# Which engine makes the low halves of weights in two sparse attentions

## The chip, the cores and the metric

The kernel runs on one core of a Trainium2 chip. The metric is the device time of one execution in microseconds (us). TensorE multiplies; ScalarE, VectorE and GpSimd prepare its operands and evacuate its results; loads and stores are issued from SyncE's queue. In the profile the engines are called PE (its weight loads PEld), ACT, DVE, POOL and SP.

## The reference

Three layers work on a sequence of 512 rows of 1024 numbers, in float32. The first two (a latent attention with its feed-forward part, a gated recurrence with its own) are not touched. The third takes a normed input h, projects it once with a wide matrix and feeds three mixers: a sparse attention that keeps 256 keys a query, chosen by a small indexer; a sparse attention over compressed, selected and windowed keys; and a state-space mixer. Each mixer's output is multiplied by a branch matrix and gated:

```python
u = h @ w_in[l]
y_a = dsa_mixer(...)      # top-k: lax.top_k(idx, n_sel), softmax over the chosen keys
y_b = nsa_mixer(...)      # 2 groups of 8 heads, three softmaxes each
y_c = ssd_mixer(...)
gates = jax.nn.sigmoid(mg.reshape(bsz, seq, 3, D_MODEL))
mix = (gates[:, :, 0] * (y_a @ w_br_dsa[l]) + gates[:, :, 1] * (y_b @ w_br_nsa[l])
       + gates[:, :, 2] * (y_c @ w_br_ssd[l]))
x = x + mix @ w_out[l]
```

## The kernel before

Every large product is made of three, so that float32 accuracy is kept: both operands are split into a high half, rounded to the matmul's input type, and a low half, the rest. `mm3` (lines 122 to 126) multiplies high by high, high by low and low by high; these are lines 124, 125 and 126 of the profile. Weights are split on the chip. `raw` (line 183) loads a piece from memory, `chunk` (line 203) makes its halves:

```python
self.nc.scalar.copy(w[:, 0], raw)
(self.nc.gpsimd if self.late and LP else self.lo).tensor_sub(w[:, 1], raw, w[:, 0])
```

So ScalarE converts (line 209), and the engine that `self.lo` names subtracts (line 210). A chunk has 128 x 1024 numbers in nearly all cases. `self.lo` also names the engine of the subtraction in `split_pair` (line 628, 128 x 512), which splits an attention's output, and of one addition in `fill_out` (line 1265), which is not reached for the first branch.

`block2` (line 1192) runs the third layer. While an attention works, TensorE also multiplies "fills": projections that a later part needs. A fill tile is one chunk, 24 products on TensorE and an evacuation. `dense_a` with `fill=True` marks its loads, chunks and evacuations as urgent: they are placed in the engines' orders as if they stood 1000 instructions earlier (`SOON`), as far as buffers allow: 3 raw pieces (`FWR`) and 2 split chunks (`FWC`). So a fill's chunk is made about two tiles ahead of its use. The order of the instructions on each engine is fixed when the program is built.

The stages around the change, in order:

- `dsa` (line 1273), prelude: the indexer (queries and keys of it are split and transposed, lines 1299 to 1313; scores and ReLU, lines 1326 to 1333), top-k by 16 rounds of MAX8 and MATCH_REPLACE for each of three blocks (lines 1336 and 1337) closed by line 1338, and `queries` for two halves of the heads (4 chunks each; transposes at line 1180). 8 of 16 gate tiles are filled ahead of the heads (`DG = 8`).
- `dsa`, heads: 16 heads in 8 pairs, each with 4 scores, a masked minimum on VectorE (line 572), exponentials on ScalarE (line 574), transposes, splits and products with the values (`pv2`). After each of the first 8 heads follows a gate tile. Each pair ends in `split_pair`.
- `nsa_group` (line 1426), run for two groups: a prelude (projection, `normed_keys` with transposes at line 1155, compression at lines 1474 to 1480, queries, the selection of blocks up to line 1557), then the fills, then 8 heads. The fills of the first group are the 8 tiles of the first branch's projection (`fill_out`), those of the second 13 tiles of z (`fill_z`, `ZN = 13`).

In the second attention `self.lo` is set by the five numbers of `NV`. The first four choose it at four places of the prelude, by `EN(nc, 1 - NV[i])`: 1 is VectorE, 0 GpSimd. The fifth is the number of fills ahead of which `self.lo` is not yet GpSimd:

```python
for f in fill[:NV[4]]:
    f()
self.lo = nc.gpsimd
for f in fill[NV[4]:n]:
    f()
```

With `NV = 1, 1, 1, 0, 0` the chunks of both preludes' own projections and queries are VectorE's, and all fills GpSimd's. From line 1207 on, and so in the whole first attention, `self.lo` is GpSimd.

Of the kernel before, what the change touches and what calls it, by code (L numbers as in the profile page):

```python
# [34 lines left out]
class Kern:  # L35
# [1156 lines left out]
    def block2(self, X, right, xp):  # L1192
        nc, A = self.nc, self.A
        self.banks(*BATT)
        self.win = win = A["w_in_2"][0]
        self.win2 = win.rearrange("(k p) n -> p k n", p=128)
        dt = lambda n, name: [self.dram.tile([128, S], F32, name=name, tag=name, bufs=n) for _ in range(n)]
        self.gd, self.zd, self.rd = dt(24, "gd"), dt(16, "zd"), [dt(8, "ra"), dt(8, "rb")]
        with ExitStack() as left:

            first = []
            self.dense_b(lambda a, b: (self.win2[:, a:b, 1024:1448], self.win2[:, a:b, 8408:8440]), X, KD, 456,
                         lambda tb, p: first.append(p), early=EF)
            self.spill_h()
            self.main.close()
            self.X2 = X
            self.lo = nc.gpsimd
            self.big = self.pool("b2", 6, left)
            self.fl = self.pool("fill", 2, left)
            self.fwr, self.fwc = self.pool("fwr", FWR, left), self.pool("fwc", FWC, left)  # L1210
            with ExitStack() as att:
                self.time_steps(first)
                self.wr, self.wc = self.pool("awr", 2, att), self.pool("awc", 2, att)
                self.dsa(X, win, first)
                self.nsa(X, win)
            self.banks(*BSSD)
            yT, rb = self.ssd(X, win, xp)
            mxp = self.pool("mxp", 4, right, side="right")
            self.wr, self.wc = (self.pool(n, b, right, side="right") for n, b in (("wor", 2), ("woc", 4)))
            mx = self.ssd_out(yT, rb, mxp)  # L1220
            self.banks(4, 2, 0, 2)

        self.lo = nc.vector
        x2 = lambda shape, dt, name: xp.tile([128] + shape, dt, name=name, tag="b8")
        self.reload_h([x2([2, D], F32, "h") for _ in range(2)])
        with ExitStack() as st:
            self.big = self.pool("big2", 8, st)
            xn = []
            bridge = self.bridge(st, None, None, A["norm2_g_2"][0], None, lambda tb: xn[tb // 2][:, tb % 2])
            xn += [x2([2, D], F32, "xn") for _ in range(2)]  # L1230
            for a in range(2):
                self.run_section(A["w_out_2"][0], a * 4, lambda k, hl: mx[a][hl][:, k], 4, self.add_to(self.H, False, 0.5),
                                 (lambda: bridge) if a else None)
            self.mlp(bridge[2], A["w_ff1_2"][0], A["w_ff2_2"][0], None, None)
# [191 lines left out]
    def nsa_group(self, X, g, gk, pos, vis, anyv, keep, addc, ltm, fill):  # L1426
        nc, A = self.nc, self.A
        with ExitStack() as st:
# [10 lines left out]
            with ExitStack() as st2:  # L1439
# [24 lines left out]

                self.lo = EN(nc, 1 - NV[0])
                self.dense_b(wsrc, X, KD, 408, evac)
                self.lo = EN(nc, 1 - NV[1])
                self.normed_keys(ip, kraw, 2, NT, lambda i: gk[:, 1 + i], lambda i: kS[i][:, 0], lambda i: kL[i][:, 0])
# [23 lines left out]
            with ExitStack() as st2:  # L1492
                ip = self.pool("cmpa", 1, st2)
                self.lo = EN(nc, 1 - NV[2])
                self.queries(ip, 1448 + g * 512, qT)
                self.lo = EN(nc, 1 - NV[3])
                pc = ip.tile([128, NT, 8, 32], F32, name="pc", **sh(SH3, "qs", 2))
# [69 lines left out]
            n = len(fill) - (NF0, NF1)[g]  # L1567
# [5 lines that stand above are left out]
# [422 lines left out]
S4 = 0  # L1995
MPN = ()
MRG = 0, 1, 2, 3
NV = 1, 1, 1, 0, 0
SH1 = 1
SH2 = 1  # L2000
SH3 = 1
# [123 lines left out]
```

## Time and profile before

| | us |
|---|---|
| time, median of 3 runs | 2748.62 (2748.05 to 2750.14) |
| profiled execution: its own time | 2748.3 |
| profiled execution: its span, first to last instruction | 2746.6 |
| the two sparse attentions in it, roughly | 1280 to 1950 |
| TensorE busy | 2652.5 |
| VectorE busy | 1619.0 |
| ScalarE busy | 1204.4 |
| GpSimd busy | 498.6 |

Times in views count from the span's start. A busy TensorE is not TensorE at its peak, since its multiplications are pipelined. [...] Idle time of an engine that nobody waits for costs nothing.

### The profile page before, as it was taken

Reading aid. Unit: us, or ns where it says so; the run is one execution under the profiler, and the core shown is the slowest. Engines: PE = TensorE matmul, PEld = TensorE weight load, DVE = VectorE, ACT = ScalarE, POOL = GpSimd, SP = SyncE. Lnnn points to the kernel's source line nnn. Section 1 sums busy time; section 2 is a strip of 40 time slices with the busy share of each in tenths; the row PEclk is TensorE's granted clock in tenths of the full one; section 3 lists DMA queues with packets and bytes.
Section 4 is the critical chain, followed back from the end, with each engine's and each line's share of the span. In section 5 each row is a group of like instructions: output and inputs, shape, how many; then the busy total and the mean of one; then the engine's idle time right before and its main releaser. Section 6 shows DMA issues by size and latency. Waiting matters only on the chain. (4 is left out here: it accounts for less than half of the span.)

```text
span 2746.6 us, 35061 instructions
## 1 busy us (share of the span) xinstructions
PE 2652.5 (97%) x13329; PEld 2192.9 (80%) x13329; DVE 1619.0 (59%) x3211; ACT 1204.4 (44%) x2382; POOL 498.6 (18%) x373
## 2 busy tenths in 40 slices
PE   8999999999998999998999999999999999999999
PEld 6888888878887888886777777777788888788887
DVE  6755444455655444457966669659557773554444
ACT  5555323335454423234367438437556552332232
POOL 1010000020002000003322213212555557100000
PEclk9999999999999999999999999999999999999999
DMA  4232223312232332233231241221353335223322
GB/s 140 62 123 77 92 93 107 109 63 84 76 116 80 99 102 92 92 119 115 89 78 59 77 109 35 62 74 36 110 155 97 112 115 169 92 92 98 101 92 77
DMA packets 281966, 259.10 MB, mean 94 GB/s; under 512 B 39436, under 2 KB 224068, under 8 KB 281796
## 3 DMA queue, kind: packets, MB, share of 16 engines
q1 hardware_dynamic: 281796, 256.84, 30.2%
q8 instruction: 105, 1.72, 0.3%
q14 instruction: 65, 0.53, 0.1%
HBM read 234.79 MB, written 22.02 MB: 94 GB/s over the span
## 5 line engine op out<-in xcount | busy, mean ns | idle before, releaser
L124 PE MATMUL pm<-xT,wch 128*128 128x512 f32 (+1 forms) x1568 | 598.1, 383 | 3.1 <-ACT xT L129 1.5
L209 ACT CAST wch<-raw 128x1024 fp32r<-128x1024 f32 (+3 forms) x389 | 402.6, 1041 | 448.1 <-PE pm L126 349.8
L126 PE MATMUL pm<-xT,wch 128*128 128x512 f32 (+1 forms) x1568 | 596.4, 381 | 1.2 <-POOL wch L210 1.2
L125 PE MATMUL pm<-xT,wch 128*128 128x512 f32 (+1 forms) x1568 | 596.7, 381 | 0.9 <-DVE xT L130 0.9
L210 POOL TENSOR_TENSOR wch<-raw,wch 128x1024 fp32r<-128x1024 f32 (+3 forms) x127 | 308.2, 2433 | 673.1 <-ACT wch L209 624.0
L210 DVE TENSOR_TENSOR wch<-raw,wch 128x1024 fp32r<-128x1024 f32 (+1 forms) x262 | 320.2, 1225 | 184.7 <-ACT wch L209 183.8
L124 PEld LDWEIGHTS pm<-xT,wch 128*128 128x128 f32 x1568 | 296.3, 190 | 55.8 <-ACT xT L129 3.2
L126 PEld LDWEIGHTS pm<-xT,wch 128*128 128x128 f32 x1568 | 297.6, 190 | 53.5 <-POOL wch L210 1.6
L125 PEld LDWEIGHTS pm<-xT,wch 128*128 128x128 f32 x1568 | 297.6, 190 | 52.0 <-DVE xT L130 2.0
L124 PE MATMUL pm<-wch,hT 128*128 128x512 f32 x768 | 300.1, 393 | 0.0
L125 PE MATMUL pm<-wch,hT 128*128 128x512 f32 x768 | 296.5, 390 | 0.0
L126 PE MATMUL pm<-wch,hT 128*128 128x512 f32 x768 | 296.4, 390 | 0.0
L529 DVE SCALAR_TENSOR_TENSOR f<-pm,r 128x512 f32<-128x512 f32 x96 | 66.4, 691 | 243.1 <-ACT r L528 242.9
L528 ACT ACTIVATE r<-pm 128x512 f32<-128x512 f32 x96 | 57.4, 598 | 315.2 <-PE pm L126 315.2
L124 PEld LDWEIGHTS pm<-wch,hT 128*128 128x128 f32 x768 | 144.3, 188 | 36.4 <-ACT hT L530 7.1
L126 PEld LDWEIGHTS pm<-wch,hT 128*128 128x128 f32 x768 | 143.6, 188 | 30.8
L125 PEld LDWEIGHTS pm<-wch,hT 128*128 128x128 f32 x768 | 144.3, 188 | 29.3
L478 POOL TENSOR_TENSOR acc<-acc,g 128x512 f32<-128x512 f32 x16 | 22.5, 1404 | 689.6 <-ACT bj L462 689.6
L574 ACT ACTIVATE p<-p,mn 128x128 f32<-128x128 f32 x224 | 125.5, 564 | 20.5 <-DVE mn L572 19.5
L440 DVE TENSOR_TENSOR acc<-pm,acc 128x512 f32<-128x512 f32 x96 | 66.1, 689 | 99.5 <-PE pm L126 99.2
L130 DVE TENSOR_TENSOR pT<-pt,pT 128x512 fp32r<-128x512 f32 x224 | 100.1, 484 | 34.7 <-ACT pT L129 32.8
L129 ACT CAST pT<-pt 128x512 fp32r<-128x512 f32 x224 | 85.3, 427 | 44.8 <-PE pt L613 30.0
(568 smaller groups left out, 4822.6 us busy)
## 6 DMA issues: line engine op xcount, KB each, us to landing
raw<-in_mlp_w_dram SPq DMA_DIRECT2D x64, 1024.0 KB, 5.2
raw<-in_w_in_dram SPq DMA_DIRECT2D x64, 512.0 KB, 3.7
raw<-in_w_ff_dram SPq DMA_DIRECT2D x32, 1024.0 KB, 5.4
raw<-in_hgrn_w_in_dram SPq DMA_DIRECT2D x24, 512.0 KB, 4.1
raw<-in_w_in_dram SPq DMA_DIRECT2D x8, 1024.0 KB, 5.0
raw<-in_w_br_ssd_dram SPq DMA_DIRECT2D x16, 512.0 KB, 4.0
gd<-fo SPq DMA_DIRECT2D x24, 256.0 KB, 2.2
fg<-gd SPq DMA_DIRECT2D x24, 256.0 KB, 3.1
```

The source lines that it names most:

```text
L124: mm(p, ah, bh, start=start, stop=False)
L125: mm(p, ah, bl, start=False, stop=False)
L126: mm(p, al, bh, start=False, stop=stop)
L129: self.nc.scalar.copy(h, src)
L130: self.nc.vector.tensor_sub(l, src, h)
L209: self.nc.scalar.copy(w[:, 0], raw)
L210: (self.nc.gpsimd if self.late and LP else self.lo).tensor_sub(w[:, 1], raw, w[:, 0])
L440: self.nc.vector.tensor_add(d, p, d)
L478: (nc.vector if tb > BP else nc.gpsimd).tensor_mul(a[:, f], a[:, f], g1[:, f])
L528: nc.scalar.activation(r, p, AF.Relu)
L529: nc.vector.scalar_tensor_tensor(f, p, 0.0, r, op0=ALU.max, op1=ALU.mult)
L574: nc.scalar.activation(p, p, AF.Exp, bias=mn[:, b:b + 1], scale=-1.0, accum_out=sm[:, b:b + 1])
```

## The change

In the first attention `self.lo` becomes VectorE. In the second, the fourth place of the prelude chooses VectorE, and the first 8 fills of each group come ahead of the switch to GpSimd: all 8 tiles of the first group, 8 of 13 of the second. After the fills of each group `self.lo` is GpSimd as before, for the `split_pair` of the second attention's heads and for the state-space mixer.

```diff
@@ -1204,7 +1204,7 @@
             self.X2 = X
-            self.lo = nc.gpsimd
+            self.lo = nc.vector
             self.big = self.pool("b2", 6, left)
@@ -1995,7 +1995,7 @@
-NV = 1, 1, 1, 0, 0
+NV = 1, 1, 1, 1, 8
```

## Rows read from the trace of the kernel before

**Rows 1.** The page's part 1: busy us, share of the span and instructions of each engine.

```profile
PE 2652.5 (97%) x13329; PEld 2192.9 (80%) x13329; DVE 1619.0 (59%) x3211; ACT 1204.4 (44%) x2382; POOL 498.6 (18%) x373
```

**Rows 2.** Windows view by stage: busy us (x instructions) of each engine, PEclk, DMA share, GB/s.

```profile
1254.00:1400.00 146.00, 128.79 (x594) 103.79 (x595) 117.68 (x289) 63.50 (x127) 45.49 (x19) 0.95 0.37 109
1400.00:1540.00 140.00, 135.89 (x758) 108.88 (x757) 88.01 (x251) 98.45 (x254) 34.82 (x57) 1.00 0.18 50
1540.00:1650.00 110.00, 100.44 (x495) 81.22 (x495) 67.55 (x155) 39.03 (x76) 22.07 (x12) 0.92 0.42 116
...
1745.00:1785.00 40.00, 34.88 (x191) 27.76 (x190) 25.78 (x74) 15.71 (x37) 10.55 (x6) 0.96 0.35 105
```

**Rows 3.** Waits of TensorE, 1250 to 1780: us in total, times, longest.

```profile
PE pt L1180 <- DVE qs L1176: 6.0, 4, 2.2
PE pt L1155 <- ACT kp L1149: 5.7, 2, 3.1
PE pt L1307 <- DVE ry L153: 5.3, 1, 5.3
PE psc L1326 <- ACT rl L1328: 3.5, 2, 1.8
PE pt L1564 <- DVE pc L1540: 2.3, 1, 2.3
...
PE pt L1155 <- DVE kp L1150: 1.6, 1, 1.6
PE pt L1307 <- DVE rt L151: 1.3, 1, 1.3
PE psc L125 <- POOL wch L210: 1.3, 1, 1.3
PE psc L1480 <- DVE bl L1476: 1.2, 1, 1.2
PE pm L126 <- POOL wch L210: 1.2, 1, 1.2
```

**Rows 4.** Timeline of GpSimd: start us, us, line, operation, tiles, count, idle time before.

```profile
1288.17 7.25 POOL L210 TENSOR_TENSOR wch<-raw,wch 128x1024 fp32r<-128x1024 f32 x3 [4.23 <-ACT wch L209]
...
1359.03 2.38 POOL L210 TENSOR_TENSOR wch<-raw,wch 128x1024 fp32r<-128x1024 f32 x1 [11.52 <-ACT wch L209]
```

**Rows 5.** Timeline of VectorE at six places.

```profile
1287.36 0.15 DVE L151 TENSOR_TENSOR rt<-ry 128x4 f32<-128x4 f32 x1
...
1288.43 2.15 DVE L152 TENSOR_TENSOR rt<-rt,rx 128x4 f32<-128x4 f32 x1
...
1317.92 2.41 DVE L1333 SCALAR_TENSOR_TENSOR dm<-rl,iw,dm 128x384 f32<-128x384 f32 x1
...
1359.46 0.69 DVE L1336 MAX8 m<-dm 128x8 f32<-128x512 f32 x1
...
1376.15 1.86 DVE L1338 TENSOR_SCALAR dm<-dm 128x512 f32<-128x512 f32 x1
...
1770.81 2.34 DVE L1476 TENSOR_SCALAR bl<-kcs,pos 128x31 f32<-128x31 f32 x1
```

**Rows 6.** Groups by line: count, busy us, mean ns, idle; page, then 1250 to 1780.

```profile
L210 DVE TENSOR_TENSOR wch<-raw,wch 128x1024 fp32r<-128x1024 f32 (+1 forms) x262 | 320.2, 1225 | 184.7 <-ACT wch L209 183.8
...
L210 POOL TENSOR_TENSOR wch<-raw,wch 128x1024 fp32r<-128x1024 f32 (+1 forms) x42 | 101.2, 2416 | 266.1 <-ACT wch L209 229.9 <-issue 16.7 <-PE pt L1180 15.3
...
L130 DVE TENSOR_TENSOR pT<-pt,pT 128x512 fp32r<-128x512 f32 x32 | 22.1, 689 | 10.0 <-ACT pT L129 9.6
```

**Rows 7.** Windows view of two stretches of VectorE.

```profile
1309.00:1377.00 68.00, 61.88 (x270) 48.46 (x269) 67.00 (x168) 23.84 (x39) 23.21 (x10) 1.00 0.29 90
1651.00:1705.00 54.00, 52.52 (x310) 42.58 (x308) 52.02 (x182) 44.16 (x133) 17.57 (x15) 1.00 0.16 45
```

**Rows 8.** ScalarE's conversions, 1250 to 1780.

```profile
L209 ACT CAST wch<-raw 128x1024 fp32r<-128x1024 f32 (+1 forms) x52 | 52.9, 1019 | 41.2 <-PE po L126 27.1 <-PE pm L126 4.9 <-DMA raw<-in_w_in_dram 4.7
```

**Rows 9.** Waits of VectorE, 1250 to 1780.

```profile
DVE wch L210 <- ACT wch L209: 25.1, 7, 6.8
```

## The prediction

> **What bounds the kernel now.** I read the page's busy table first: TensorE is busy 97% of 2746.6 us, GpSimd 18% [rows 1]. Time is gained only where TensorE is idle or slow, so the next view is the windows table, cut at the edges of the stretch that the change reaches: the prelude of the first attention (indexer, top-k, queries), its heads, and the two preludes of the second attention's groups [rows 2]. TensorE's idle time is length minus its busy time: 17.2 us, 4.1, 9.6 and 5.1. The heads run nearly without gaps; the preludes lose. In the three preludes the granted clock is also down, 0.95, 0.92 and 0.96 in the mean. [...]
>
> Then who ends TensorE's waits in this stretch [rows 3]. The ten rows shown add up to 29.4 us. Only 2.5 of them name GpSimd's low halves. Most name a small VectorE operation, or ScalarE's conversion behind one: the reader is to ask why small operations are late. The timelines of GpSimd and VectorE, laid side by side, answer it [rows 4, 5]. A 128x4 operation on VectorE takes 0.15 us at 1287.36 and 2.15 at 1288.43, where a GpSimd subtraction began at 1288.17; a 128x31 one takes 2.34 at 1770.81. Each ends as the subtraction beside it ends. MAX8 at 1359.46 takes its 0.69 us although GpSimd subtracts from 1359.03. So some VectorE operations stand still while GpSimd works on a chunk, and top-k doesn't. Of the 40 chunks that move, 17 have one such stalled operation or more beside them; the 17 stalled operations, the first at 1288.43 and the last at 1770.81, are some 28 us above their usual times, and four of which only one or a few exist (a mask copy, a clamp, two closings of top-k, one of them the 1.86 us at 1376.15) some 6 more. TensorE's longest wait, 5.3 us for the indexer's transposes, follows three of them.
>
> **What moves.** In the first attention: 8 chunks of the queries, 16 of gate tiles and 8 subtractions of 128x512 on its outputs. In the second: 8 chunks of the first branch's projection and z tiles 0 to 7. The fills are made ahead, so in time these are the 40 chunks from 1279 to 1771; z tiles 8 to 12, from 1782 on, stay on GpSimd. No load moves to another queue, no wait is added by name; each subtraction's wait for ScalarE's conversion moves onto VectorE's queue.
>
> **Prices.** A 128x1024 subtraction takes GpSimd 2.42 us and VectorE 1.23; a 128x512 one takes VectorE 0.69 [rows 6]. GpSimd loses 40 x 2.42 = 97 us and the eight smaller ones; that gives nothing by itself, since it was 18% busy. VectorE gains 40 x 1.23 + 8 x 0.69 = 54.7 us of work and loses about 34 us of standing still: 21 us more in all. What counts is where.
>
> *Preludes, gain.* A stall of 1.5 to 2.3 us ahead of a waiting TensorE is replaced, at worst, by a subtraction of 1.23 us in the same place. If it always is, roughly half of the wait goes; if the subtraction falls into VectorE's own idle time, nearly all. For GpSimd's own two waits the price is halved as well. I take half, the nearest row being the subtraction itself: 29.4 / 2 = 14.7 us. The ends are 5 (only where stall and subtraction differ most) and 25.
>
> *Clock.* The stretches with gaps are those with a lowered mean clock; the first heads keep 1.00 [rows 2]. Some gaps should become too short for a drop; which ones no row tells. Ends are 0 and 15 of the 17.7; I take 7.
>
> *Top-k, cost.* From 1309 to 1377 VectorE is busy 67.0 of 68 us [rows 7], so here nothing covers a new subtraction. Ten chunks fall into it: 12.3 us, less 5.9 of four stalls there (from 1317.92 to 1376.15, [rows 5]), so top-k would end 6.4 us later; it also starts earlier, since the three stalled operations before it lose 5.6 and get at most 3.7. TensorE meanwhile has gates and queries to multiply. Ends 0 and 6.4; I take 3.
>
> *First heads of the second attention, cost.* From 1651 to 1705 VectorE is busy 52.0 of 54 [rows 7] and two chunks fall in, a third just before it: 3.7 us with no stall taken away. I take 3, ends 0 and 3.7.
>
> *Heads of the first attention, cost.* Seven chunks and eight subtractions, 7 x 1.23 + 8 x 0.69 = 14.1 us, on an engine busy 88.0 of 140 [rows 2]. Other work covers them, but softmax behind one waits up to 1.23 us. I take 2; ends 0 and 7 (half).
>
> *The loads' buffers.* A raw buffer comes free when its subtraction ends, 1.2 us sooner if VectorE is free. Hidden by three fill buffers: 0. If that cover goes, it shows as the queue wait of the first rival.
>
> Sum: -14.7 - 7 + 3 + 3 + 2 = -13.7. Against the profiled execution's 2748.3 us (span 2746.6) that is 2734.6; the median of the runs shown is 0.3 above that execution, so **2735**.
>
> [...]
>
> **Rivals.**
>
> *VectorE becomes the bound, through its queue* (15%, **2760**). For: 13 chunks fall into stretches without cover [rows 7], and a subtraction at the head of the queue waits for ScalarE's conversion, 1.02 us [rows 8], with softmax and top-k behind it. The subtractions VectorE already makes in this stretch found it idle before them for 25.1 us in 7 waits [rows 9]. Price: 13 x (1.23 + 1.02) = 29.2, less 5.9 of stalls, less half of the 24.6 us of waits that lie outside (29.4 without the scores' 3.5 and one of GpSimd's 1.3), no clock gain: +11.0. Against: none of TensorE's ten waits names a subtraction that VectorE makes today [rows 3]. It decides from about 1 us of new waiting per chunk. [...]
>
> *Nothing to measure* (20%, **2748**). The subtraction lands where the stall was, the fills' multiplications follow the same conversions, no clock drop goes: 14.7 falls to some 8, and the three costs take 8 back.
>
> *Nearly all comes back* (12%, **2720**). Subtractions fall into idle VectorE time; 80% of the waits (23.5) and 13 of the clock go, 8 is paid.
>
> **How the numbers follow.** The forecast's case has 53%; its time is the prediction. Its own range is 2727 to 2744. About 0.2%, or 5.5 us, is what a measurement of this kernel can tell. Faster: nearly all of 53 plus 12, less what lies within 5.5, makes 0.63; same 0.20; slower 0.17, the first rival and the tail of the second. The range goes from 2720 to 2756: it takes in the third rival's time and the second's, and leaves out most of the first.
>
> **What would show it.** Right: 40 more VectorE subtractions of about 1.23 us, no 2 us operation on small VectorE shapes from 1279 to 1771; the 5.3 us wait at the indexer's transposes under 2.5; TensorE's waits for queries' and keys' transposes about halved; granted clock in the preludes up by 0.02 or more; z tiles 8 to 12 with stalls as before; top-k ending no more than 3 us later, counted from its start. Wrong: VectorE's waits for conversions rising by over 20 us, TensorE's idle time in the heads over 10 us, or stalls that stay without GpSimd's subtractions, which would mean that their cause is another.

## The result and the profile after

The changed kernel takes **2718.02 us** (median of 4 runs, 2715.64 to 2720.55) beside 2748.34 us (2746.04 to 2750.14) of the kernel before: ratio 0.9886, 95% interval [0.9873, 0.9898], so 30.3 us less. The forecast was 2735, its range 2720 to 2756: the direction was right, but the time lies 2 us below the range, and the gain was more than twice the 13.7 us of the sum.

The page's part 1 of the kernel after (it answers to [rows 1]) gives the first account:

```profile
span 2713.6 us, 35052 instructions
...
PE 2641.3 (97%) x13329; PEld 2182.9 (80%) x13329; DVE 1636.8 (60%) x3259; ACT 1205.7 (44%) x2382; POOL 396.4 (15%) x325
```

TensorE makes the same 13329 matmuls. Its busy time fell from 2652.5 to 2641.3 us, 11.2 less, because less of the work ran at the lower clock: the mean granted clock of the span, as a share of full speed, rose from 0.989 to 0.994. In windows of 1 us the three preludes of the kernel before show 0.50 or 1.00, and values between only next to a change from one to the other. Behind the 5.3 us wait of [rows 3], at 1297.38, a 128x512 product took 0.63 us (0.50 from 1293 to 1299), at 1300.38 one took 0.39 (1.00 from 1300 to 1302). Its idle time, span less busy, fell from 94.1 to 72.3 us, 21.8 less. Together that is the 33.0 us by which the two spans differ; some 3.5 of them lie ahead of the changed stretch, where nothing differs, and the medians are 30.3 apart. Counted from the last transposes ahead of that stretch (L399, at 1273.96 and 1270.47), 21.1 us are idle time and 8.4 are clock. The table of all kernels below is split by whole spans.

Where it went is seen in the windows by stage of the kernel after (it answers to [rows 2], cut where the stages lie now: prelude and heads of the first attention, first and second prelude of the second one; columns as there):

```profile
1251.00:1395.00 144.00, 141.64 (x662) 114.65 (x663) 124.47 (x311) 67.27 (x131) 0.00 (x0) 0.99 0.45 130
1395.00:1530.00 135.00, 131.53 (x752) 107.82 (x750) 98.48 (x267) 98.07 (x259) 8.72 (x42) 1.00 0.13 35
1530.00:1635.00 105.00, 102.72 (x544) 82.35 (x542) 76.91 (x207) 48.47 (x101) 3.97 (x5) 1.00 0.49 134
1745.00:1785.00 40.00, 37.25 (x201) 29.36 (x202) 18.36 (x56) 10.56 (x20) 3.42 (x3) 0.91 0.30 93
```

TensorE's idle time in the first two preludes is 2.4 and 2.3 us, where it was 17.2 and 9.6, and their granted clock 0.99 and 1.00 instead of 0.95 and 0.92. The heads between them lose 3.5 us, before 4.1. The last prelude, where GpSimd goes on, keeps a lowered clock (0.91; before 0.96).

The waits of TensorE from 1250 to 1780 (it answers to [rows 3]; us in total, times, longest), the seven largest, and the two that name a low half or the indexer's transposes:

```profile
PE pt L1155 <- ACT kp L1149: 6.4, 3, 3.5
PE pt L399 <- DVE acc L494: 1.9, 1, 1.9
PE po L618 <- ACT pT L129: 1.5, 4, 0.7
PE pt L1180 <- DVE qs L1176: 1.3, 3, 0.8
PE psc L1326 <- ACT rl L1328: 1.0, 1, 1.0
PE psc L1363 <- DVE mn L572: 0.8, 2, 0.5
PE pt L1564 <- DVE pc L1540: 0.8, 1, 0.8
...
PE pm L126 <- DVE wch L210: 0.2, 1, 0.2
...
PE pt L1307 <- DVE ry L153: 0.2, 1, 0.2
```

The 5.3 us at the indexer's transposes (L1307) are 0.2, the queries' 6.0 are 1.3, the scores' 3.5 are 1.0, and no wait names GpSimd. Only the keys' transposes (L1155) kept theirs; of the 6.4 us 5.7 lie from 1745.50 on, in the prelude where GpSimd goes on. The ten waits of [rows 3], 29.4 us, come to 9.9.

The longest of the waits, 5.3 us, lay between the first and the second transposes of the indexer (L1307 at 1287.59 and 1296.18). In the kernel before three operations stood still there; the first is in [rows 5], the other two and the last step to the second transposes (L1304) are

```profile
1291.38 1.64 DVE L153 SCALAR_TENSOR_TENSOR ry<-rt,ry 128x4 f32<-128x4 f32 x1
...
1293.15 2.29 DVE L151 TENSOR_TENSOR rt<-ry 128x4 f32<-128x4 f32 x1
...
1295.82 0.22 DVE L1304 TENSOR_TENSOR ipk<-psc,ipk 128x64 fp32r<-128x64 f32 x1
```

The same operations on VectorE in the changed kernel (start, us):

```profile
1284.43 0.15 DVE L152 TENSOR_TENSOR rt<-rt,rx 128x4 f32<-128x4 f32 x1
1284.50 2.35 DVE L210 TENSOR_TENSOR wch<-raw,wch 128x1024 fp32r<-128x1024 f32 x2
1286.77 0.22 DVE L1304 TENSOR_TENSOR ipk<-psc,ipk 128x64 fp32r<-128x64 f32 x1
1286.91 0.15 DVE L153 SCALAR_TENSOR_TENSOR ry<-rt,ry 128x4 f32<-128x4 f32 x1
...
1289.50 1.22 DVE L210 TENSOR_TENSOR wch<-raw,wch 128x1024 fp32r<-128x1024 f32 x1
1290.64 0.22 DVE L1304 TENSOR_TENSOR ipk<-psc,ipk 128x64 fp32r<-128x64 f32 x1
```

L152 takes 0.15 us, not 2.15. Two subtractions stand ahead of the first transposes for 2.35 us, and TensorE waits 0.2 us for those. Between the first and the second transposes stands one subtraction of 1.22 us, where three stalled operations took 6.08: from one L1304 to the next it was 8.6 us (1287.22 to 1295.82) and is 3.9. So not every stall got a subtraction in its place.

VectorE itself: 40 more subtractions at the same price, and more idle time ahead of them (groups by line, whole kernel; then its waits from 1250 to 1780, which answer to [rows 9]):

```profile
L210 DVE TENSOR_TENSOR wch<-raw,wch 128x1024 fp32r<-128x1024 f32 (+1 forms) x302 | 368.8, 1224 | 187.3 <-ACT wch L209 186.6
```

```profile
DVE wch L210 <- ACT wch L209: 37.9, 16, 7.0
```

### The profile page after: what moved, and what is told of

It is laid out like the page before. It is cut to its first block, busy times and chain, and to the rows that moved or that the text cites. A ratio compares the mean times of both kernels' runs of the same rounds, so it can differ in the third digit from the quotient of the medians.

```text
span 2713.6 us, 35052 instructions
## 1 busy us (share of the span) xinstructions
PE 2641.3 (97%) x13329; PEld 2182.9 (80%) x13329; DVE 1636.8 (60%) x3259; ACT 1205.7 (44%) x2382; POOL 396.4 (15%) x325
## 4 chain that ended last, share of the span: by engine, by line
PE 83%; DVE 9%; ACT 4%; DMA 1%; issue 1%; POOL 0%; SPq 0%; DVEq 0%; ACTq 0%; POOLq 0%
PE pm L124 21%; PE pm L125 21%; PE pm L126 21%; PE po L618 2%; PE psc L124 2%; PE psc L125 2%; PE psc L126 2%; PE psc L1912 1%; PE pt L613 1%; PE psc L1072 1%; DVE wch L210 1%; DMA na<-in_ssd_a_log_dram 1%; PE pt L399 1%; DVE acc L494 1%; ACT wch L209 1%
## 5 line engine op out<-in xcount | busy, mean ns | idle before, releaser
L209 ACT CAST wch<-raw 128x1024 fp32r<-128x1024 f32 (+2 forms) x389 | 402.6, 1041 | 451.8 <-PE pm L126 351.4
L210 DVE TENSOR_TENSOR wch<-raw,wch 128x1024 fp32r<-128x1024 f32 (+1 forms) x302 | 368.8, 1224 | 187.3 <-ACT wch L209 186.6
L210 POOL TENSOR_TENSOR wch<-raw,wch 128x1024 fp32r<-128x1024 f32 (+3 forms) x87 | 212.3, 2446 | 432.5 <-ACT wch L209 403.6
L574 ACT ACTIVATE p<-p,mn 128x128 f32<-128x128 f32 x224 | 125.9, 565 | 21.4 <-DVE mn L572 20.1
L130 DVE TENSOR_TENSOR pT<-pt,pT 128x512 fp32r<-128x512 f32 x224 | 101.0, 485 | 21.2 <-ACT pT L129 19.0
L129 ACT CAST pT<-pt 128x512 fp32r<-128x512 f32 x224 | 86.4, 426 | 44.9 <-PE pt L613 29.4
```

Source lines behind the costliest of these rows:

```text
L129: self.nc.scalar.copy(h, src)
L130: self.nc.vector.tensor_sub(l, src, h)
L574: nc.scalar.activation(p, p, AF.Exp, bias=mn[:, b:b + 1], scale=-1.0, accum_out=sm[:, b:b + 1])
```

## The experiments

Three theories stood at the start. **Theory 1**: VectorE stands still while GpSimd reads beside it, TensorE waits and its clock drops; the change takes that away. **Theory 2**: with other engines for 40 subtractions the order of all instructions came out different (compared in the traces by line and tile, 520 of 13329 matmuls stand elsewhere), and that order is luckier. **Theory 3**: GpSimd made the low halves too late for the products.

| kernel | us | ratio to before, 95% | span | TensorE busy | idle |
|---|---|---|---|---|---|
| before | 2748.3 | | 2746.6 | 2652.5 | 94.1 |
| changed | 2718.0 | 0.9886 [0.9873, 0.9898] | 2713.6 | 2641.3 | 72.3 |
| first part alone | 2731.0 | 0.9939 [0.9924, 0.9954] | 2726.7 | 2646.1 | 80.6 |
| second part alone | 2735.4 | 0.9958 [0.9942, 0.9975] | 2734.6 | 2646.7 | 87.9 |
| changed, GpSimd reads beside | 2791.6 | 1.016 [1.0145, 1.0175] | 2790.5 | 2664.7 | 125.8 |
| changed, GpSimd writes beside | 2768.6 | 1.0076 [1.0061, 1.0091] | 2767.2 | 2657.2 | 110.0 |
| before, GpSimd only writes | 2715.3 | 0.9874 [0.9859, 0.9888] | 2713.3 | 2641.3 | 72.0 |
| changed, 13 z tiles | 2712.6 | 0.9863 [0.9848, 0.9877] | 2709.6 | 2640.7 | 68.9 |
| changed, all later halves | 2709.6 | 0.9858 [0.9841, 0.9874] | 2707.6 | 2641.5 | 66.1 |
| changed, earlier halves | 2703.3 | 0.9829 [0.9815, 0.9844] | 2702.0 | 2636.4 | 65.6 |
| earlier halves, 13 z tiles | 2696.1 | 0.9811 [0.9798, 0.9825] | 2694.2 | 2633.8 | 60.4 |
| no low half on GpSimd | 2696.4 | 0.9814 [0.9801, 0.9827] | 2694.0 | 2635.7 | 58.3 |

Each ratio is to the kernel before as it was timed again beside that kernel; its median was 2747.3 beside the two parts and the two kernels with added work, 2748.4 beside the last two rows and 2751.7 beside the other four experiments.

### The two parts of the change, each alone

In the kernel before, the first:

```diff
-            self.lo = nc.gpsimd
+            self.lo = nc.vector
```

> The first attention's part alone (gates, queries, the eight subtractions on its outputs). Theory 1, standing still: VectorE's small operations no longer stand still beside GpSimd's subtractions, and TensorE's gaps and half-level stretches of the first prelude go; by the traces the end of the first attention came 19.8 us sooner, some 3 of which arose ahead of the change, so 16 to 20 us: 2728 to 2732 us. The second prelude keeps its gaps of about 9.6 us. Theory 2, a luckier order: the two parts need not add up; with the order only half changed the gain may be anything from 0 to 30 us.

The second:

```diff
-NV = 1, 1, 1, 0, 0
+NV = 1, 1, 1, 1, 8
```

> The second attention's part alone (its first branch's projection and z tiles 0 to 7). Theory 1: the second prelude's gaps of 9.6 us fall to about 2.3 and its half-level stretches go (at most 8.8 us), the first prelude keeps its 17.2 us of gaps: 10 to 14 us less than before, 2734 to 2738 us, and the gains of the two parts add up to some 30 us. Theory 2: they don't add up.

Measured: 2731.03 and 2735.41 beside 2747.33, so 16.3 and 11.9 us less. Their sum is 28.2, near the 30.3 of both together. The windows of the first prelude and of the first one of the second attention, first part alone:

```profile
1251.00:1395.00 144.00, 139.85 (x657) 112.69 (x657) 126.36 (x311) 66.17 (x129) 2.25 (x1) 1.00 0.44 127
1530.00:1635.00 105.00, 93.62 (x473) 74.06 (x472) 68.27 (x159) 39.26 (x76) 23.96 (x12) 0.95 0.45 124
```

and second part alone:

```profile
1251.00:1395.00 144.00, 125.71 (x586) 101.06 (x587) 118.86 (x289) 63.46 (x127) 44.66 (x20) 0.96 0.38 110
1530.00:1635.00 105.00, 103.15 (x546) 83.65 (x545) 66.93 (x163) 42.26 (x81) 3.97 (x5) 1.00 0.46 125
```

Each part clears its own prelude, in idle time and in granted clock, and leaves the other's as it was: 11.4 us idle at 0.95 in the one, 18.3 at 0.96 in the other. In the two of these windows in which GpSimd (the fifth) is busy 24.0 and 44.7 us the prelude loses, in the two with 2.3 and 4.0 it loses 4.2 and 1.9 us at 1.00. The 8.8 us of the second expectation are an estimate from [rows 2], 0.08 x 110. Both times are within theory 1's ranges. Gains that add up speak against a lucky order, but they don't tell theory 1 from theory 3.

### GpSimd's work put back, beside the change

Both kernels are the changed one with work for GpSimd after each of the 40 moved chunks, into a tile that nobody uses. The first reads the chunk's high half:

```diff
+    for c in range(0, 1024, 384):
+        k = min(384, 1024 - c)
+        self.nc.gpsimd.tensor_sub(o[:, :k], a[:, c:c + k], a[:, c:c + k])
```

> The changed kernel, and beside each of the 40 moved chunks GpSimd subtracts the chunk's high half from itself into a tile that nobody uses (added work, 40 x about 2.5 to 2.9 us). Nothing waits for its result. Theory 1: VectorE stands still beside it as before, and more often, for it now makes the subtractions too: most of the 30 us comes back, 2738 to 2755 us, with VectorE operations of 1.5 to 2.9 us on small shapes in both preludes. Theory 3, GpSimd is only slow (2.42 us against 1.23, and the products wait for it): nothing waits for the added work, so 2716 to 2722 us.

The second only writes, after ScalarE has copied one column of the chunk, so that the writing starts no sooner:

```diff
+    self.nc.scalar.copy(o[:, 0:1], a[:, 0:1])
+    for _ in range(6):
+        self.nc.gpsimd.memset(o, 0.0)
```

> The changed kernel, and for each of the 40 moved chunks GpSimd writes constants over a tile that nobody uses, about as long as it would subtract, but reads nothing; ScalarE copies one column per chunk besides (added work). Theory 1 in its narrow form, two readers of the memory get in each other's way: 2716 to 2722 us and no small VectorE operation of 2 us in the two preludes. In its wide form, any work of GpSimd on the memory stops VectorE: as with the added subtractions, 2738 to 2755 us. If only the shifted order of instructions matters, both runs with added work move by the same amount.

Measured: 2791.62 and 2768.64 us. Both are above every figure that was given. The common part is a thing that no theory had foreseen: in both, TensorE waits 19.3 us at one place of the first prelude, for the evacuation of the indexer's scores. The waits of the reading kernel and of the writing one, 1250 on, begin with the same row:

```profile
PE psc L1326 <- ACT rl L1328: 25.1, 11, 19.3
```

The changed kernel has 1.0 us there. With the added instructions the others came out in another order: 410 of TensorE's matmuls stand elsewhere than in the changed kernel. So neither time may be read against 2718. The two may be read against each other: between them 14 matmuls and 2 VectorE operations stand elsewhere, and GpSimd's added work is nearly as long (124.0 us of subtractions, 101.0 of writing). The reading kernel takes **23.0 us** more than the writing one. VectorE's and GpSimd's timelines at the queries' 128x512 operations show what reading does. Reading, VectorE and then GpSimd:

```profile
1380.76 1.32 DVE L1173 TENSOR_TENSOR qraw<-qraw,ry 128x512 f32<-128x512 f32 x1
1382.00 2.33 DVE L1176 TENSOR_TENSOR qs<-qraw,qs 128x512 fp32r<-128x512 f32 x2
```

```profile
1380.28 3.50 POOL L2107 TENSOR_TENSOR ghost<-wch 128x384 f32<-128x384 f32 x3 [14.38 <-ACT wch L209]
```

Writing, the same two:

```profile
1380.18 0.68 DVE L1173 TENSOR_TENSOR qraw<-qraw,ry 128x512 f32<-128x512 f32 x1
1380.78 1.29 DVE L1176 TENSOR_TENSOR qs<-qraw,qs 128x512 fp32r<-128x512 f32 x2
```

```profile
1380.84 1.37 POOL L2107 MEMSET ghost<- 128x384 f32 x3 [16.00 <-ACT ghost L2105]
```

Two of the same operations take 2.33 us beside GpSimd's subtractions and 1.29 beside its writes. But not all of the 23.0 us is such standing still. The added subtraction also keeps the chunk's buffer until it has read it, which the writing doesn't: in the reading kernel ScalarE's conversions wait for that in two places.

```profile
ACT wch L209 <- POOL ghost L2107: 8.4, 2, 6.1
```

These lie at 1396.77 and 1400.13, ahead of TensorE's wait of 8.5 us for the queries at 1418.27, which in the writing kernel is 1.9. How the 23.0 us divide is open. The pair shows that the reading slows VectorE; as a measure of the gain it failed.

### The kernel before, with GpSimd writing in place of subtracting

This takes only the reading away. In the 40 chunks GpSimd subtracts one column and then writes a constant over the low half twice, so it is nearly as late with each chunk as before (86.3 us for the 40, where the subtractions took some 97), VectorE gets no new work, and the order changes less (86 matmuls stand elsewhere than before, not 520). The low halves' values are left out of these 40 products.

```diff
+    l = w[:, 1].bitcast(F32)
+    self.nc.gpsimd.tensor_sub(w[:, 1, 0, 0:1], raw[:, 0, 0:1], w[:, 0, 0, 0:1])
+    for _ in range(2):
+        self.nc.gpsimd.memset(l, 1e-6)
```

> The kernel before, in nearly its own order, but for the 40 chunks GpSimd subtracts one column and then writes a constant over the low half twice, about 2.4 us in all as before (the low halves' values are left out). GpSimd is as late with each chunk as before and VectorE gets no new work; only GpSimd's reading is gone. Theory 1, VectorE stands still beside GpSimd's reading: the gain comes without the change's move, 2714 to 2728 us, no small VectorE operation of 2 us in the two preludes, and what the result lies under the changed kernel's 2718 is the price of VectorE's 55 us of new work. Theory 3, the low halves came too late from GpSimd: nothing is sooner, 2743 to 2752 us. Theory 2, the changed kernel's other order made the gain: 2740 to 2752 us.

Measured: **2715.25 us** (2714.99 to 2716.70), ratio 0.9874. GpSimd is busy 488.1 us, nearly as before, and VectorE, the third, less than before:

```profile
PE 2641.3 (97%) x13329; PEld 2180.2 (80%) x13329; DVE 1590.8 (59%) x3211; ACT 1206.5 (44%) x2382; POOL 488.1 (18%) x453
```

TensorE's busy time is that of the changed kernel, its idle time 72.0 beside 72.3. That they agree to some tenths is partly chance: up to the last transposes ahead of the stretch (L399) the profiled execution of the changed kernel is 3.2 us shorter than this one, though nothing differs there, and behind them it is 3.5 us longer. The windows of the two preludes:

```profile
1251.00:1395.00 144.00, 138.81 (x658) 112.28 (x657) 111.08 (x309) 69.54 (x137) 42.52 (x58) 0.99 0.42 119
...
1530.00:1635.00 105.00, 101.24 (x544) 80.37 (x543) 72.36 (x213) 50.97 (x111) 24.95 (x33) 1.00 0.46 124
```

With GpSimd busy as before, TensorE is idle for 5.2 and 3.8 us, not 17.2 and 9.6. At the indexer's small operations the timelines of VectorE and GpSimd read:

```profile
1287.69 0.15 DVE L152 TENSOR_TENSOR rt<-rt,rx 128x4 f32<-128x4 f32 x1
...
1288.02 0.16 DVE L153 SCALAR_TENSOR_TENSOR ry<-rt,ry 128x4 f32<-128x4 f32 x1
```

```profile
1287.37 0.20 POOL L2102 TENSOR_TENSOR wch<-raw,wch 128x1 fp32r<-128x1 f32 x1 [3.79 <-ACT wch L209]
1287.62 2.06 POOL L2104 MEMSET wch<- 128x1024 f32 x2
```

0.15 us inside GpSimd's 2.06, where before it was 2.15 [rows 4, 5]. Theory 3 falls: the low halves come only about a quarter of a microsecond sooner each, not 1.2, and the whole gain is there. Theory 2 falls as the main cause. It is clearest in the second attention's first prelude, where 9 matmuls alone stand elsewhere than before and the idle time falls from 9.6 to 3.8 us. In the first prelude the order does have a part: between the first two transposes (L1307) TensorE has 19 products, not 13, and at the 0.23 us from one to the next there the six more cover 1.4 of the 5.3 us; what the order gives at that prelude's shorter waits was not separated. Theory 1 stands for most of the gain: L152 takes 0.15 us beside GpSimd's writes and 2.15 beside its subtraction.

The run also prices the move. The changed kernel has some 55 us more VectorE work in these stretches (40 x 1.22 and 8 x 0.69, prices of [rows 6]), and its time is 2718.0 against 2715.3; the ratios' intervals overlap. So the subtractions cost some 3 us, and perhaps nothing. It is no exact price, since in the writing kernel the eight smaller subtractions stay on GpSimd and its order is another.

### What is left on GpSimd

If the theory holds, every further low half taken from GpSimd should pay where TensorE waits. Five kernels, from the changed one: z tiles 8 to 12 as well (`NV = 1, 1, 1, 1, 13`); that and no return to GpSimd for the second attention's outputs and the state-space branch's chunks (line 1570 removed); the earlier stages' halves (`LP = 0`) alone; and two with both.

> The changed kernel with all 13 z tiles on VectorE. Theory 1: of the gaps left in the second group's prelude (some 14 us in six gaps, beside VectorE operations that stand still for 12 us) about half go: 2709 to 2716 us. A rival, VectorE is the bound there by now: 2717 to 2724 us.

> The changed kernel with all z tiles, the second attention's output halves and the chunks of the state-space branch on VectorE: GpSimd makes no low half after the first attention's start. Theory 1: the rest of the standing still goes as well, 2690 to 2712 us. The rival, that VectorE becomes the bound in the stretch behind the attentions (it is 60 to 90% busy there in many slices, and more than 50 chunks of 1.23 us are added): 2720 to 2760 us.

> The changed kernel with the low halves that GpSimd makes in the earlier stages (some 18 chunks, among them four of 2.4 us just ahead of the first attention, beside which VectorE stands still for 7.3 us) on VectorE. Theory 1: where TensorE waits behind such an operation it gains, 2712 to 2718 us; the rival, that the cover there is enough or VectorE is busier: 2717 to 2725 us.

Measured: 2712.64, 2709.63 and 2703.30 us. The first two are within theory 1's ranges. The z tiles' run clears the last prelude: TensorE's waits from 1735 on have 0.4 us at L1155 (5.7 in the changed kernel), and the second group's heads begin 9.0 us sooner, of which 4.0 are left at the end. The third gained 14.7 us, more than twice what was expected at best, and lies below its range. Most of its gain lies ahead of the first attention, whose indexer comes 8.7 us sooner. The largest piece is the norms' last operation (L494), whose results TensorE transposes next. In the view of one tile's operations (duration in ns: least, median, longest) the changed kernel has

```profile
L494 DVE SCALAR_TENSOR_TENSOR acc<-h,ry,g x32: 739/752/2846, 215.0 to 1261.8; 128x512 f32<-128x512 f32 x32
```

and this one

```profile
L494 DVE SCALAR_TENSOR_TENSOR acc<-h,ry,g x32: 743/747/753, 215.2 to 1252.5; 128x512 f32<-128x512 f32 x32
```

TensorE's waits for it over the whole run, first there, then here:

```profile
PE pt L399 <- DVE acc L494: 10.4, 8, 2.1
```

```profile
PE pt L399 <- DVE acc L494: 2.4, 4, 1.0
```

So the same stall was at work in the layers before, which the prediction left aside.

> GpSimd makes no low half any more: the earlier stages' on VectorE too, and those of the run with all of the later ones there. Theory 1: the two gains lie in different stretches (14.7 us and 8.4 us under the changed kernel's 2718.0) and add up: 2692 to 2699 us. The rival, that they share a cause further on or VectorE binds: 2700 to 2706 us.

> The earlier stages' low halves and all 13 z tiles on VectorE, the state-space branch's chunks on GpSimd as before. Theory 1: 14.7 and 5.4 us add up, 2695 to 2701 us. If VectorE's load behind the attentions is what limits the run without any GpSimd halves, this one is the faster of the two.

Measured: 2696.35 and 2696.14 us, which can't be told apart; both are within theory 1's ranges. 14.7 and 5.4 do add up (21.9 measured, 20.1 expected). Moving the more than 50 chunks behind the attentions as well takes VectorE to 62% and gives nothing further on top. Against before the better one is 0.9811 [0.9798, 0.9825], 52 us.

## Why the prediction was right in direction and short by half

*The reading of the stall was right.* "Some VectorE operations stand still while GpSimd works on a chunk, and top-k doesn't" is what the writing kernel shows as the cause of most of the gain: without GpSimd's 40 subtractions L152 takes 0.15 us, not 2.15, and the span falls from 2746.6 to 2713.3. The rows that carried it were [rows 4, 5].

*"Preludes, gain", half of 29.4: this step failed.* It held that a stall of 1.5 to 2.3 us "is replaced, at worst, by a subtraction of 1.23 us in the same place", and charged half of every wait for that. The ten waits fell to 9.9 us: 19.5 went, not 14.7, and 5.7 of what is left stand in the prelude where GpSimd goes on. In the kernel that has hardly a stall and no new subtraction the same ten come to 8.7. So the subtractions cost TensorE some 1 us of these waits. At the longest wait one subtraction of 1.22 us came in the place of three stalls of 6.08 together, and TensorE had 16 products between the two transposes, enough to cover the 3.9 us.

Where subtractions did come right ahead of a transpose, 2.35 us of them at the first L1307, TensorE waited 0.2 us. Why is argued here, not shown: the order is fixed when the program is built, and it may put other products ahead of a transpose whose operands will be late by work that it knows. A subtraction on VectorE is such work; standing still beside GpSimd is not. That the changed kernel, ordered anew, has no gap there fits this. The 19.3 us wait of the two kernels with added work shows that another order can lose far more; what in the added instructions led to that order was not tried.

*"Clock", 7 of 17.7: nearly right.* No run shows a loss of 17.7 us; it is an estimate, what the mean clocks of [rows 2] lack to 1.00 times the lengths (0.05 x 146, 0.08 x 110 and 0.04 x 40). In its place the runs showed busy time fall by 11.2 us, of which 8.4 in the changed stretch. The granted clock of the two preludes is 0.99 and 1.00, where it was 0.95 and 0.92; that it would have stayed lower with gaps only halved is not shown.

*The three costs, 8 us: near 0, from the same premise.* Top-k did get longer, from 66.7 us to 75.1 (first MAX8 to the last L1338), so 8.3, more than the 6.4 worked out. But nobody waited: in the writing kernel the last L1338 comes at 1363.4, 14.1 us sooner than the changed kernel's 1377.5, and the last products of the first attention's heads (L618) end at 1516.6 and 1515.6. "TensorE meanwhile has gates and queries to multiply" was in the text; the 3 us charged against it were not due. In the first attention's heads TensorE lost 3.5 us instead of 4.1 + 2. In all, gain less costs was put at 6.7 us of idle time; 21.1 were measured.

*The rivals.* "Nearly all comes back" (12%, 2720) came within 2 us, in part by luck: it took 23.5 us of the ten waits (19.5 went) and 13 of the clock (8.4 to 11.2), and paid 8 us that weren't due. Its condition, subtractions in idle VectorE time, holds for some of them only: the 2.35 us ahead of L153 had no idle time before them. "VectorE becomes the bound" didn't happen: VectorE is busy 60%, its waits for conversions rose by 12.8 us [rows 9], not by the 20 that were named as the sign, and those are idle time of VectorE: it came to its subtractions early. "Nothing to measure" is out by its own condition, since the clock drops of the two preludes went (0.95 and 0.92 before, 0.99 and 1.00 after). Taking work from GpSimd to VectorE made the kernel faster with both parts of the change (by 16.3 and 11.9 us), top-k's stretch with its saturated VectorE [rows 7] among them, and with the earlier stages' halves (14.7 us); behind the attentions it made no difference (2696.35 us with, 2696.14 without).

*The signs that were named.* Right: the subtractions' 1.22 us, the wait at L1307 under 2.5, the queries' waits at least halved, the clock up by over 0.02, the second group's prelude with stalls as before (three operations of some 2.4 us from 1735 to 1756, beside the z tiles' subtractions; ahead of them no small operation of 2 us is left). Wrong: the keys' waits (L1155) were not halved, and top-k took more than 3 us longer.

## What to carry to other kernels

Where VectorE's small operations show durations many times their usual (here 2.15 us, not 0.15), lay GpSimd's timeline beside them: here the helper's subtractions cost more by what they stopped (some 30 us) than their move to VectorE did (some 3), and its low busy share (18%) didn't tell. When such a stall is removed, don't charge the moved work in its place without asking who waits for it: here 55 us of moved work cost some 3 us, and about 34 us of stalls had cost some 30. To separate standing still from lateness and from order, let the helper write for as long as it read, and check how much of the order is still the same, above all at the longest wait.

## What was not expected of the hardware

- GpSimd's kind of work decided, not its time: in the 40 chunks 76.6 us of writes and 9.7 of subtracting one column, in place of some 97 us of subtractions, were worth 33 us of the span (2746.6 to 2713.3).
- TensorE's gaps cost more than their length here: of the 33.0 us between the spans of the kernel before and the changed one, 21.8 were idle time and 11.2 busy time, with products of 0.63 us at a granted clock of 0.50 and of 0.39 at 1.00.
- Some small operations stayed long with writes too. In the kernel where GpSimd only writes, a 128x8 operation with one operand and constants took 0.98 us, where one of the next kind took 0.17:

```profile
1538.51 0.98 DVE L146 TENSOR_SCALAR rx<-rx 128x8 f32<-128x8 f32 x1
...
1539.53 0.17 DVE L152 TENSOR_TENSOR rt<-rt,rx 128x8 f32<-128x8 f32 x1
```

That a write of GpSimd held it is the author's estimate, from the durations alone: the writes at 1282.63 and 1545.07 took 0.95 us each. TensorE's idle time in that kernel is 72.0 us, that of the changed one 72.3.
